# First two k-tiles of the in-projection as plain float32 products, part of the first modulation summed on TensorE, and in-projection passes that run to and fro

## The chip, the cores and the metric

The kernel runs on one core of a Trainium2 chip. The metric is the device time of one execution in microseconds (us). TensorE (PE in the rows) does the matrix products, VectorE (DVE) and ScalarE (ACT) do the elementwise work, GpSimd (POOL) a little of it, and SyncE (SP) issues nearly all DMA transfers. Weights come from HBM; products are summed in the eight banks of PSUM, and everything else lives in SBUF.

## The reference, cut to what matters

One transformer block on 256 tokens of width 2048, all in float32, with modulation vectors computed from a condition vector `c`:

```
mod = silu(c) @ w_ada + b_ada                       # 2048 x 12288
shift_m, scale_m, gate_m, shift_f, scale_f, gate_f = split(mod, 6)
h = rms_norm(x, pre_norm_mix) * (1 + scale_m) + shift_m
q_n, k_c, v_c, k_s, v_s, k_w, v_w, g_n, q_m, k_m, v_m = split(h @ w_in)   # 2048 x 5656
o = concat(nsa_mixer(...), moba_mixer(...)) @ w_o
x = x + gate_m * rms_norm(o, post_norm_mix)
h = rms_norm(x, pre_norm_ffn) * (1 + scale_f) + shift_f
x = x + gate_f * rms_norm(square(relu(h @ w_up)) @ w_down, post_norm_ffn)
```

The change touches the start: `silu(c)`, `shift_m` and `scale_m`, and `h @ w_in`.

## The kernel before

**Products.** A float32 product runs as three products in the faster fp32r format: each operand is split into a high part (`hi`, a cast on ACT) and the rest (`lo`, a subtraction on DVE), and `products` issues hi x hi, hi x lo and lo x hi. K is cut into 16 k-tiles of 128 rows. The 5656 columns of `w_in` form six blocks: `kv`, `qn`, `qm`, `km`, `vm` of 1024 columns and `kw` of 536. For one k-tile and one block of 1024 columns there are two token tiles x two halves of 512 columns x three products = 12 products; the four sums lie in four PSUM banks. Five banks (`mbank`) serve these sums, three (`bank`) the rest.

**Passes.** All k-tiles cannot run at once, since their modulation is not known yet. So the in-projection runs in passes: k-tiles 0 to 3 of all six blocks, 4 to 7 of all six, 8 to 11 of `qm` and `km`, then 8 to 15 of `kv`, `kw`, `qn`, 12 to 15 of `qm` and `km`, and 8 to 15 of `vm`. After each pass of a block its four banks are evacuated: copied out by ACT the first time, added to the earlier sum by DVE (line 573) after that.

**Modulation.** `mod_units` makes shift and scale for a group of k-tiles (`M_MODS`, four groups of four). Their columns of `w_ada` (4 x 128 for shift, 4 x 128 for scale) are loaded for all 16 k-tiles of `c`, and DVE multiplies each of these 16 blocks of 128 x 1024 by a column of `silu(c)` and adds it up (line 310, a SCALAR_TENSOR_TENSOR). Eight transposes on PE and two sums on DVE (line 347) then add over the partitions, POOL adds the bias and multiplies by the gain (lines 351, 353), ACT applies shift and scale to the transposed x (line 372) and casts the high part, and DVE makes the low part. The groups for the next pass are worked out during a pass (`spread`).

**Order.** `Stream` emits units (a load, a preparation, a use) in a fixed order. Loads go through five buffers of 1 MB (`rawtile`); a buffer is free when the preparation has read it, and SP issues the loads in order, so one load that waits for its buffer holds up all later ones. The five split weight tiles (`whi`, `wlo`) form a second limit. Each engine's own queue is written by a scheduler and runs strictly in order.

Of the kernel before, what the change touches and what calls it, by code (L numbers as in the profile page):

```python
# [12 lines left out]
F32 = mybir.dt.float32  # L13
F32R = mybir.dt.float32r
# [61 lines left out]
class Stream:  # L76
    """Emits units in order; loads and preparations run ahead as far as the buffers reach."""
# [56 lines left out]
def spread(base, extra, first, last):  # L134
    """The units of base with the groups in extra placed between positions first and last."""
# [17 lines left out]
def tile_adaln_block(ctx: ExitStack, tc: tile.TileContext, x, c, w_ada, b_ada, g_pm, g_qm, w_in,  # L153
# [28 lines left out]
    # Constants  # L182
    ident = cp.tile([P, P], F32, name="ident")
    make_identity(nc, ident)
    onesr = cp.tile([P, P], F32R, name="onesr")
    nc.scalar.activation(onesr, ident, AF.Identity, bias=1.0, scale=0.0)
    identb = cp.tile([P, P], BF16, name="identb")
    nc.vector.tensor_copy(identb, ident)
    sel4 = cp.tile([P, 32], F32, name="sel4")
    nc.vector.tensor_add(sel4, ident[:, 0:32], ident[:, 32:64])  # L190
    nc.vector.tensor_add(sel4, sel4, ident[:, 64:96])
    nc.vector.tensor_add(sel4, sel4, ident[:, 96:128])
    mhalf = cp.tile([P, 1], F32, name="mhalf")
    nc.gpsimd.memset(mhalf, -0.5)

    maskf = accp.tile([P, NT, NCMP + T], F32, tag="acc", name="maskf")
    nc.gpsimd.memset(maskf, 0.0)
    for t in range(NT):
        nc.gpsimd.affine_select(
            out=maskf[:, t, 0:NCMP], in_=maskf[:, t, 0:NCMP], compare_op=ALU.is_ge, fill=NEG,  # L200
            base=t * P - (CLEN - 1), pattern=[[-CSTR, NCMP]], channel_multiplier=1)
        nc.gpsimd.affine_select(
            out=maskf[:, t, NCMP:], in_=maskf[:, t, NCMP:], compare_op=ALU.is_ge, fill=NEG,
            base=t * P, pattern=[[-1, T]], channel_multiplier=1)
    mask = cp.tile([P, NT, NCMP + T], BF16, name="mask")
    nc.vector.tensor_copy(mask, maskf)

    rp = cp.tile([P, NT, 2, HD], F32, name="rp")

# [7 lines left out]
    nc.scalar.dma_start(stageb[0:32, :], ck_pos[0])  # L217
    nc.scalar.dma_start(stageb[32:64, :], cv_pos[0])
# [7 lines left out]
    cola = cp.tile([P, P], F32, name="cola")  # L226
    colb = cp.tile([P, 80], F32, name="colb")
    pc = bank("pconst0")
    nc.tensor.transpose(pc[:, 0:16], stagec, ident[0:16, 0:16])
    nc.scalar.copy(colb[:, 0:16], pc[:, 0:16])  # L230
    pb = bank("pconst")
    nc.tensor.transpose(pb[:, 0:64], stageb, ident[0:64, 0:64])
    nc.scalar.copy(colb[:, 16:80], pb[:, 0:64])
    pa = bank("pconst2")
    nc.tensor.transpose(pa[:, 0:P], stagea, ident)
    nc.scalar.copy(cola, pa[:, 0:P])
    for i in (1, 4):
        scale = cola[:, i * KD:(i + 1) * KD]
# [1021 lines left out]
```

## Time and profile before

| | us |
|---|---|
| time, three runs | 1200.81, 1201.71, 1202.43 (median 1201.71) |
| span of the profiled execution, first to last instruction | 1199.2 |
| TensorE busy | 1140.5 (95%) |
| VectorE busy | 908.5 (76%) |
| ScalarE busy | 602.2 (50%) |
| DMA | 312 MB, 260 GB/s on average |

The profiled execution is listed by its span alone; the median of the timed runs is 2.5 us above it. Busy shares are averages over stages with different limits. The in-projection fills about the first 280 us; the output projection and the FFN follow, and there TensorE is busy nearly all the time.

### The profile page before, as it was taken

To read this page: it belongs to the slowest core of one execution; us is meant where nothing else is said; L and a number is where in the kernel's file an instruction comes from. 1 tells how busy PE (TensorE), PEld (TensorE's weight loads), DVE (VectorE), ACT (ScalarE), POOL (GpSimd) and SP (SyncE) were. 2 spreads that over 40 slices of the span, in tenths; PEclk is the share of its full clock that TensorE was granted. 3 is DMA by queue.
4 is the path that set the end of the run, shared out by engine and by line. 5 is a ranking of instruction groups with operands and counts; after the bars stand their busy time and mean duration, and the time that the engine had idled before them with its cause. 6 is when DMAs were issued, how large, how long until landed. Compare 5 with 4: busy or idle time off the path is not lost.

```text
span 1199.2 us, 14451 instructions
## 1 busy us (share of the span) xinstructions
PE 1140.5 (95%) x5429; PEld 935.9 (78%) x5429; DVE 908.5 (76%) x1086; ACT 602.2 (50%) x922; POOL 32.7 (3%) x38
## 2 busy tenths in 40 slices
PE   2599998999999999999999999999999999999997
PEld 1477886878778887888888788888888888888885
DVE  6877999879998897876988986757666666665564
ACT  3446343436756666665343344767544444444441
POOL 1000001000000031000000000000000000000000
PEclk9699999999999999999999999999999999999999
DMA  9898989886766695997867875555677767775541
GB/s 334 311 392 277 361 307 336 261 293 246 273 223 233 246 356 178 360 333 276 315 250 279 315 266 193 176 176 187 215 258 268 259 253 274 253 278 178 207 142 70
DMA packets 88249, 312.02 MB, mean 260 GB/s; under 512 B 6051, under 2 KB 6515, under 8 KB 75251
## 3 DMA queue, kind: packets, MB, share of 16 engines
q1 hardware_dynamic: 87876, 311.01, 72.6%
q8 instruction: 42, 0.69, 0.2%
q14 instruction: 27, 0.21, 0.0%
q10 hardware_dynamic: 304, 0.11, 0.0%
HBM read 308.99 MB, written 2.10 MB: 259 GB/s over the span
## 4 chain that ended last, share of the span: by engine, by line
PE 81%; DVE 9%; issue 3%; DMA 3%; ACT 2%; POOL 1%; DVEq 0%; POOLq 0%; ACTq 0%
PE dps L498 9%; PE dps L496 9%; PE dps L497 9%; PE up L496 9%; PE up L498 9%; PE up L497 9%; DVE modm L310 3%; PE wo L496 2%; PE wo L498 2%; PE wo L497 2%; PE ft L1083 1%; PE in_vm L497 1%; PE in_vm L498 1%; PE in_vm L496 1%; PE in_kv L496 1%
## 5 line engine op out<-in xcount | busy, mean ns | idle before, releaser
L310 DVE SCALAR_TENSOR_TENSOR modf<-modf,csil,modf 128x1024 f32<-128x1024 f32 x60 | 76.7, 1278 | 9.2 <-DMA modf<-in_w_ada_dram 9.1
L310 DVE SCALAR_TENSOR_TENSOR modm<-modm,csil,modm 128x1024 f32<-128x1024 f32 x60 | 76.8, 1280 | 0.9
L1099 DVE TENSOR_TENSOR facc<-up,facc 128x512 f32<-128x512 f32 x96 | 61.5, 683 | 18.7 <-PE up L498 18.7
L310 DVE SCALAR_TENSOR_TENSOR gatef<-gatef,csil,gatef 128x1024 f32<-128x1024 f32 x32 | 40.6, 1278 | 1.3 <-DMA gatef<-in_w_ada_dram 1.3
L310 DVE SCALAR_TENSOR_TENSOR gatem<-gatem,csil,gatem 128x1024 f32<-128x1024 f32 x32 | 40.2, 1273 | 0.0
L1139 DVE TENSOR_TENSOR flo<-facc,fhi 128x512 fp32r<-128x512 f32 x32 | 21.7, 684 | 2.0 <-ACT fhi L1138 2.0
L1138 ACT CAST fhi<-facc 128x512 fp32r<-128x512 f32 x32 | 19.7, 624 | 5.3 <-PE up L497 1.9
L1101 ACT ACTIVATE facc<-facc 128x512 f32<-128x512 f32 x32 | 18.4, 624 | 2.8 <-DVE facc L1099 2.8
L1097 ACT COPY facc<-up 128x512 f32<-128x512 f32 x32 | 17.8, 594 | 1.6 <-PE up L498 1.0
L492 DVE TENSOR_TENSOR up_13lo<-up,up_13hi 128x1024 fp32r<-128x1024 f32 x8 | 9.8, 1226 | 11.5 <-ACT up_13hi L491 11.5
L492 DVE TENSOR_TENSOR up_14lo<-up,up_14hi 128x1024 fp32r<-128x1024 f32 x8 | 9.8, 1224 | 11.1 <-ACT up_14hi L491 11.1
L345 PE MATMUL modm0t<-ident,modm 128*128 128x128 f32 x8 | 1.9, 424 | 17.0 <-DVE modm L310 17.0
L1088 ACT ACTIVATE facc<-ft 128x512 f32<-128x512 f32 x32 | 17.2, 588 | 0.4 <-PE ft L1083 0.2
L1083 PE MATMUL ft<-ident,facc 128*128 128x128 f32 x128 | 16.8, 273 | 0.0
L1083 PEld LDWEIGHTS ft<-ident,facc 128*128 128x128 f32 x128 | 14.7, 140 | 2.6 <-ACT facc L1088 0.5
L492 DVE TENSOR_TENSOR up_0lo<-up,up_0hi 128x1024 fp32r<-128x1024 f32 x8 | 9.8, 1223 | 7.7 <-ACT up_0hi L491 7.7
L491 ACT CAST up_7hi<-up 128x1024 fp32r<-128x1024 f32 x8 | 8.4, 1056 | 14.3 <-PE up L498 14.3
L491 ACT CAST up_11hi<-up 128x1024 fp32r<-128x1024 f32 x8 | 8.4, 1055 | 14.2 <-PE up L498 14.2
L351 POOL TENSOR_TENSOR modf0red<-modf0red,cola 128x8 f32<-128x8 f32 x1 | 9.0, 8993 | 227.3 <-ACT wo_15hi L491 227.3
L491 ACT CAST up_10hi<-up 128x1024 fp32r<-128x1024 f32 x8 | 8.4, 1056 | 13.3 <-PE up L498 13.3
L491 ACT CAST up_6hi<-up 128x1024 fp32r<-128x1024 f32 x8 | 8.4, 1055 | 13.3 <-PE up L498 13.3
L345 PEld LDWEIGHTS modm0t<-ident,modm 128*128 128x128 f32 x8 | 1.6, 224 | 17.2 <-ACT in_kv_1hi L491 17.2
(2340 smaller groups left out, 4020.2 us busy)
## 6 DMA issues: line engine op xcount, KB each, us to landing
up<-in_w_up_dram SPq DMA_DIRECT2D x64, 1024.0 KB, 6.6
dn<-in_w_down_dram SPq DMA_DIRECT2D x64, 1024.0 KB, 4.9
modm<-in_w_ada_dram SPq DMA_DIRECT2D x64, 512.0 KB, 6.5
modf<-in_w_ada_dram SPq DMA_DIRECT2D x64, 512.0 KB, 5.9
gatem<-in_w_ada_dram SPq DMA_DIRECT2D x16, 1024.0 KB, 4.9
wo<-in_w_o_dram SPq DMA_DIRECT2D x16, 1024.0 KB, 5.3
gatef<-in_w_ada_dram SPq DMA_DIRECT2D x16, 1024.0 KB, 4.8
in_kv<-in_w_in_dram SPq DMA_DIRECT2D x8, 1024.0 KB, 7.3
```

Source lines behind the costliest of these rows:

```text
L310: nc.vector.scalar_tensor_tensor(part, w[:, j:j + step], csil[:, k:k + 1], part, ALU.mult, ALU.add)
L491: nc.scalar.copy(hi[:, 0:n], src)
L492: nc.vector.tensor_sub(lo[:, 0:n], src, hi[:, 0:n].bitcast(F32))
L496: nc.tensor.matmul(o, shi, whi, start=first, stop=False)
L497: nc.tensor.matmul(o, shi, wlo, start=False, stop=False)
L498: nc.tensor.matmul(o, slo, whi, start=False, stop=last)
L1083: nc.tensor.transpose(b[:, (2 * i + t) * P:(2 * i + t + 1) * P], f[:, t, (2 * j + i) * P:(2 * j + i + 1) * P], ident)
L1097: nc.scalar.copy(dst, b)
L1099: nc.vector.tensor_add(dst, b, dst)
L1101: nc.scalar.activation(dst, dst, AF.Relu)
L1138: nc.scalar.copy(hi, f)
L1139: nc.vector.tensor_sub(lo, f, hi.bitcast(F32))
```

## The change

- `M_MODS` becomes (2, 2, 4, 4, 4). The first two groups are two k-tiles wide, so their blocks are 128 x 512; four k-tiles of `c` share one buffer, loaded by four DMAs of 256 KB in place of two of 512 KB.
- In the first group the blocks of k-tiles 3, 7, 11, 13 and 15 of `c` (`M_DIRECT`) are not added on DVE: TensorE multiplies them by the column of `silu(c)` (`column_sums`), which adds over the partitions at once. All groups of the mixer now end with such products by a column of ones instead of transposes, with the bias added by one more product, and two small DVE operations follow. The later FFN groups keep the transposes, with bias and gain on DVE instead of POOL.
- k-tiles 0 and 1 (`M_PLAIN` = 2) of all blocks are multiplied as plain float32: no cast, no subtraction, one product in place of three. Their loaded buffer is held until TensorE has used it.
- The passes are now: k-tiles 0 and 1 of `kv`, `kw`, `qn`, `vm`, `km`, `qm`; then 2 and 3 in the order `qm` (its banks kept from the pass before), `km`, `vm`, `qn`, `kw`, `kv`; then `kv` on through 4 to 7 in the same banks, `kw`, `qn`, `vm`, `km`, and `qm` 4 to 11 in one go, `km` 8 to 11. From `kv` 8 to 15 on the order is that of before.
- At the start the constants for the mixer (mask, `sel4`, compressed positions) are loaded and made later, and the path from `c` to `silu(c)` is shorter.

```
-M_MODS = (4, 4, 4, 4)
+M_MODS = (2, 2, 4, 4, 4)
+M_PLAIN = 2
+M_DIRECT = (3, 7, 11, 13, 15)
...
                 for kk in range(krows):
                     k = i * krows + kk
                     w = st["raw"][:, kk * n:(kk + 1) * n]
+                    if direct is not None and k in M_DIRECT:
+                        direct(k, w)
+                        continue
...
+        def column_sums(w, v, stop):
+            if "b" not in sums:
+                sums["b"] = bank(f"{name}t")
+                nc.tensor.matmul(sums["b"][:, 0:2 * nk].rearrange("p (s k) -> p s k", s=2), ident,
+                                 bias[:, :, ks], start=True, stop=False, skip_group_check=True)
+            for i in range(2 * nk):
+                nc.tensor.matmul(sums["b"][:, i:i + 1], w[:, i * P:(i + 1) * P], v,
+                                 start=False, stop=stop, skip_group_check=True)
...
+                column_sums(acc.t, one, True)
+                b = sums["b"]
+                nc.vector.tensor_mul(red[:, nk:], b[:, nk:2 * nk], gcol[:, ks])
+                nc.vector.tensor_copy(red[:, 0:nk], b[:, 0:nk])
...
+                        if k < plain:
+                            nc.tensor.matmul(b[:, 0:wd], s32,
+                                             raw[:, kk * ncol + off:kk * ncol + off + wd],
+                                             start=first, stop=last)
+                        else:
+                            products(b[:, 0:wd], shi, slo, whi[:, cs], wlo[:, cs], first, last)
...
+    turn0 = in_units("qm", 0, 4)
+    turn1 = in_units("kv", 2, 8)
+    turn2 = in_units("qm", 4, 12)
+    stream.add(flat(mods[0]))
+    base = flat(in_units(n, 0, 2) for n in ("kv", "kw", "qn", "vm", "km")) + turn0[:2]
+    stream.add(spread(base, mods[1], 3, len(base) - 1))
+    base = turn0[2:] + flat(in_units(n, 2, 4) for n in ("km", "vm", "qn", "kw")) + turn1[:2]
+    base.insert(3, Unit(None, late_constants))
+    stream.add(spread(base, mods[2], 0, len(base) - 2))
+    base = turn1[2:] + flat(in_units(n, 4, 8) for n in ("kw", "qn", "vm", "km")) + turn2[:4]
+    stream.add(spread(base, mods[3], 0, len(base) - 5))
+    base = turn2[4:] + in_units("km", 8, 12)
```

Three places show how the queues move. The first is TensorE's queue from the last transposes of x to the first products of the in-projection (`modm0t` is the bank of the first modulation group, `xnm` the modulated x, `in_kv_0_0` the bank of the first half of `kv` for the first token tile). Before:

```order
L274 MATMUL xt_3_269<-ident,x_150 128x128 x4
L345 MATMUL modm0t_316<-ident,modm_192 128x128 x4
L345 MATMUL modm0t_322<-ident,modm_192 128x128 x4
L496 MATMUL in_kv_0_0_346<-in_kv_0hi,modm0hi_332 128x512
L497 MATMUL in_kv_0_0_346<-in_kv_0lo,modm0hi_332 128x512
L498 MATMUL in_kv_0_0_346<-in_kv_0hi,modm0lo_333 128x512
```

After the change the same place reads:

```order
L283 MATMUL xt_3_280<-ident,x_121 128x128 x4
L359 MATMUL modm0t<-csil,modm_138 128x1 x4
L356 MATMUL modm2t<-cola,ident 128x4
L359 MATMUL modm0t<-csil,modm_143 128x1 x4
L359 MATMUL modm0t<-csil,modm_148 128x1 x8
L359 MATMUL modm0t<-one,modm_175 128x1 x4
L497 MATMUL in_kv_0_0_306<-in_kv_0_153,xnm_211 128x512
L497 MATMUL in_kv_1_0_308<-in_kv_0_153,xnm_211 128x512
```

The eight transposes have become products with one column, and the first product of the in-projection reads the loaded weight and x directly.

The second place is SP's queue, from the loads of the first modulation group to the sixth load of weights or modulation behind it (`modm` is modulation, `in_kv`, `in_kw` and so on are weights of the in-projection). Before:

```order
L295 DMA modm_205<-in_w_ada_dram 128x2x512 x2
L433 DMA in_kv_0_246<-in_w_in_dram 128x2x1024
L433 DMA in_kv_2_278<-in_w_in_dram 128x2x1024
L433 DMA in_kw_0_282<-in_w_in_dram 128x2x536
L295 DMA modm_286<-in_w_ada_dram 128x2x512 x2
L433 DMA in_kw_2_291<-in_w_in_dram 128x2x536
L295 DMA modm_301<-in_w_ada_dram 128x2x512 x2
```

After:

```order
L305 DMA modm_148<-in_w_ada_dram 128x2x256 x4
L476 DMA in_kv_0_153<-in_w_in_dram 128x2x1024
L476 DMA in_kw_0_185<-in_w_in_dram 128x2x536
L305 DMA modm_194<-in_w_ada_dram 128x2x256 x4
L305 DMA modm_206<-in_w_ada_dram 128x2x256 x4
L476 DMA in_qn_0_257<-in_w_in_dram 128x2x1024
L305 DMA modm_292<-in_w_ada_dram 128x2x256 x4
L476 DMA in_vm_0_318<-in_w_in_dram 128x2x1024
```

The group ahead of the first product is four buffers of 1 MB instead of eight (before, `modm_157` to `modm_205`), and weights of one pair of k-tiles alternate with the next group.

The third place is where the plain pass ends: `km` 0 and 1 is the pass's fifth block, `qm` 2 the first weights that are split. ACT's queue there, after the change:

```order
L629 COPY km_441<-in_km_0_1_411 128x512
L629 COPY km_444<-in_km_1_1_413 128x512
L544 CAST in_qm_2hi<-in_qm_2_384 128x1024
L544 CAST in_qm_3hi<-in_qm_2_384 128x1024
L544 CAST in_km_2hi<-in_km_2_450 128x1024
```

And DVE's queue at the same place, after the change (`modm_415` is the sum of the third group):

```order
L323 SCALAR_TENSOR_TENSOR modm_415<-modm_363,csil,modm_415 128x1024
L545 TENSOR_TENSOR in_qm_2lo<-in_qm_2_384,in_qm_2hi 128x1024
L323 SCALAR_TENSOR_TENSOR modm_415<-modm_404,csil,modm_415 128x1024
L545 TENSOR_TENSOR in_qm_3lo<-in_qm_2_384,in_qm_3hi 128x1024
L323 SCALAR_TENSOR_TENSOR modm_415<-modm_404,csil,modm_415 128x1024
L323 SCALAR_TENSOR_TENSOR modm_415<-modm_418,csil,modm_415 128x1024 x2
L545 TENSOR_TENSOR in_km_2lo<-in_km_2_450,in_km_2hi 128x1024
L323 SCALAR_TENSOR_TENSOR modm_415<-modm_454,csil,modm_415 128x1024
L545 TENSOR_TENSOR in_km_3lo<-in_km_2_450,in_km_3hi 128x1024
L323 SCALAR_TENSOR_TENSOR modm_415<-modm_454,csil,modm_415 128x1024
L631 TENSOR_TENSOR km_441<-in_km_0_0_561,km_441 128x512
L323 SCALAR_TENSOR_TENSOR modm_415<-modm_469,csil,modm_415 128x1024 x2
```

The casts stand behind the copies that evacuate `km`, so DVE's second row there waits for TensorE to finish that block; and the first addition of a bank (line 631) now stands between two steps of the third group's sum.

## Rows read from the trace of the kernel before

**Rows 1.** The page: busy time by engine; TensorE's granted clock by slice.

```profile
PE 1140.5 (95%) x5429; PEld 935.9 (78%) x5429; DVE 908.5 (76%) x1086; ACT 602.2 (50%) x922; POOL 32.7 (3%) x38
PEclk9699999999999999999999999999999999999999
```

**Rows 2.** Windows: stretch, length, busy time by engine, granted clock, DMA share, GB/s.

```profile
15.00:38.00 23.00, 5.66 (x34) 4.97 (x33) 21.36 (x20) 6.88 (x18) 1.59 (x1) 0.72 1.04 392
50.00:123.00 73.00, 69.53 (x329) 57.01 (x328) 57.89 (x55) 38.79 (x57) 2.17 (x2) 1.00 0.93 337
123.00:200.00 77.00, 72.90 (x341) 59.38 (x340) 75.07 (x81) 29.58 (x32) 2.18 (x2) 1.00 0.92 337
200.00:250.00 50.00, 47.33 (x271) 39.83 (x273) 45.01 (x77) 21.67 (x30) 4.01 (x3) 1.00 0.77 255
250.00:1100.00 850.00, 846.28 (x4042) 693.82 (x4041) 643.60 (x770) 454.81 (x712) 16.71 (x13) 1.00 0.72 257
```

**Rows 3.** Timeline from the start to the first products: start, duration, instruction.

```profile
4.98 2.13 SPq L519 DMA_DIRECT2D x<-in_x_dram  x4
9.72 1.06 ACT L525 ACTIVATE xj<-x 128x1024 f32<-128x1024 f32 x1 [4.78 <-DMA x<-in_x_dram]
14.98 0.74 DVE L305 TENSOR_SCALAR modm<-modm,csil 128x1024 f32<-128x1024 f32 x1
...
37.42 1.94 PE L345 MATMUL modm0t<-ident,modm 128*128 128x128 f32 x8 [17.00 <-DVE modm L310]
44.59 0.79 PE L496 MATMUL in_kv<-in_kv_0hi,modm0hi 128*128 128x512 f32 x1 [5.24 <-ACT modm0hi L375]
48.94 0.39 PE L497 MATMUL in_kv<-in_kv_0lo,modm0hi 128*128 128x512 f32 x1
```

**Rows 4.** TensorE's timeline at two places: plain float32 products, then fp32r products.

```profile
316.95 0.59 PE L743 MATMUL on<-pt,ksv 128*128 128x256 f32 x2
317.38 0.38 PE L744 MATMUL on<-pt,ksv 128*128 128x128 f32 x2
...
274.78 0.39 PE L496 MATMUL in_qm<-in_qm_13hi,modm12hi 128*128 128x512 f32 x1
275.01 0.39 PE L497 MATMUL in_qm<-in_qm_13lo,modm12hi 128*128 128x512 f32 x1
```

**Rows 5.** DVE's timeline between 121 and 201 us, cut to one row of each kind.

```profile
121.81 0.69 DVE L573 TENSOR_TENSOR kcv<-in_kv,kcv 128x512 f32<-128x512 f32 x1 [0.39 <-PE in_kv L498]
130.94 1.46 DVE L573 TENSOR_TENSOR wide<-in_kw,wide 128x268 f32<-128x268 f32 x4
132.32 1.21 DVE L492 TENSOR_TENSOR in_qn_6lo<-in_qn,in_qn_6hi 128x1024 fp32r<-128x1024 f32 x1
133.45 1.27 DVE L310 SCALAR_TENSOR_TENSOR modm<-modm,csil,modm 128x1024 f32<-128x1024 f32 x1
134.64 1.22 DVE L492 TENSOR_TENSOR in_qn_7lo<-in_qn,in_qn_7hi 128x1024 fp32r<-128x1024 f32 x1
155.72 0.69 DVE L376 TENSOR_TENSOR modm8lo<-xnm,modm8hi 128x512 fp32r<-128x512 f32 x1 [1.62 <-ACT modm8hi L375]
166.96 0.74 DVE L305 TENSOR_SCALAR modm<-modm,csil 128x1024 f32<-128x1024 f32 x1
198.00 1.22 DVE L492 TENSOR_TENSOR in_km_11lo<-in_km,in_km_11hi 128x1024 fp32r<-128x1024 f32 x1
```

**Rows 6.** TensorE's timeline where `kv` 8 begins.

```profile
199.57 0.39 PE L497 MATMUL in_km<-in_km_11lo,modm8hi 128*128 128x512 f32 x1
202.50 0.39 PE L496 MATMUL in_kv<-in_kv_8hi,modm8hi 128*128 128x512 f32 x1
```

**Rows 7.** ScalarE's timeline: one cast of a weight, one copy of a bank.

```profile
44.95 1.03 ACT L491 CAST in_kv_2hi<-in_kv 128x1024 fp32r<-128x1024 f32 x1
...
55.75 0.59 ACT L571 COPY kcv<-in_kv 128x512 f32<-128x512 f32 x1
```

**Rows 8.** Window of 2 us in which loads with runs of 512 B (`w1k`) land.

```profile
238.00:240.00 2.00, 2.00 (x15) 1.80 (x14) 2.00 (x6) 1.08 (x2) 0.00 (x0) 1.00 1.06 292
```

More of the change, by code (lines that the diff above doesn't have):

```diff
@@ L180, in rawtile, with sigmoid_parts @@
         return wp.tile([P, 2048], F32, tag="raw", bufs=RAWBUFS, name=name)
+    def sigmoid_parts(dst, src):
+        nc.vector.tensor_scalar(dst, src, -87.0, None, ALU.max)
+        nc.scalar.activation(dst, dst, AF.Exp, scale=-1.0)
+        nc.vector.tensor_scalar(dst, dst, 1.0, None, ALU.add)
     ident = cp.tile([P, P], F32, name="ident")
     make_identity(nc, ident)
[L185 to L192, printed above, removed]
     mhalf = cp.tile([P, 1], F32, name="mhalf")
     nc.gpsimd.memset(mhalf, -0.5)
[L196 to L208, printed above, removed]
+    one = cp.tile([P, 1], F32, name="one")
+    nc.gpsimd.memset(one, 1.0)
+    cola = cp.tile([P, P], F32, name="cola")
+    colb = cp.tile([P, 64], F32, name="colb")
+    csil = cp.tile([P, KD], F32, name="csil")
     stagea = accp.tile([P, P], F32, tag="acc", name="stagea")
@@ L277, in transposed, with gemv_units @@
                                b[:, j * 256:(j + 1) * 256].rearrange("p (k q) -> p k q", k=2))
-    def gemv_units(name, c0, width, both, krows, acc, first):
+    def gemv_units(name, c0, width, both, krows, acc, first, direct=None):
         units = []
@@ L334, in first @@
                 acc.t = gp.tile([P, 2 * W], F32, tag="ga", name=name)
-        units = gemv_units(name, base + k0 * P, W, True, 2 if W <= 512 else 1, acc, first)
+        ks = slice(k0, k0 + nk)
+        sums = {}
+        def column_sums(w, v, stop):
[6 more added lines that the diff above has]
+                                 start=False, stop=stop, skip_group_check=True)
@@ new lines, in reduce @@
+            if tag == "f" and k0:
+                with tc.high_priority():
+                    for i0 in range(0, 2 * nk, 4):
+                        n = min(4, 2 * nk - i0)
+                        b = bank(f"{name}t{i0}")
+                        for i in range(n):
+                            nc.tensor.transpose(b[:, i * P:(i + 1) * P],
+                                                acc.t[:, (i0 + i) * P:(i0 + i + 1) * P], ident)
+                        nc.vector.tensor_reduce(red[:, i0:i0 + n],
+                                                b[:, 0:n * P].rearrange("p (k q) -> p k q", k=n),
+                                                axis=AX.X, op=ALU.add)
+                    nc.vector.tensor_add(red.rearrange("p (s k) -> p s k", s=2),
+                                         red.rearrange("p (s k) -> p s k", s=2), bias[:, :, ks])
+                    nc.vector.tensor_mul(red[:, nk:], red[:, nk:], gcol[:, ks])
+                return lambda k: (red[:, k - k0:k - k0 + 1], red[:, nk + k - k0:nk + k - k0 + 1])
@@ L569, in done @@
                 dst = acc[n][:, t, :]
-            if g == 0:
+            if (name, ci, t) not in begun:
+                begun.add((name, ci, t))
                 nc.scalar.copy(dst, b[:, 0:wd])
@@ L908, in tile_adaln_block @@
     mods = [mod_units("m", k0, n, xnm, hstat) for k0, n in zip(k0s, M_MODS)]
-    stream.add([x_units(0), x_units(1)])
+    xu = [x_units(0), x_units(1)]
+    columns()
+    stream.add(xu)
     gm = gate_units("m", g_qm, gate_m)
```

170 lines of the change are left out of this document (86 added, 84 removed).

## The prediction

> **What bounds the kernel now.** I read the page first: TensorE is busy for 95% of the span and at its full clock in every slice of 30 us but the second [rows 1]. So there is little to win except where TensorE stands still, and the windows say where that is. From 250 to 1100 us it is busy for 846 of 850 us; up to 38 us it has hardly begun; from 50 to 250 it loses 3.5, 4.1 and 2.7 us in the three stretches [rows 2]. The change touches nothing after the in-projection that TensorE waits for, so I ask one question: how much earlier does TensorE reach a place behind which both programs are alike? That place is the first product of `kv` 8, at 202.50 us [rows 6].
>
> Next I looked for what sets the pace up to there. The timeline of the start shows the sum of the first modulation group: DVE begins it at 14.98, TensorE waits for it 17 us, sums at 37.42 and has its first product at 44.59 [rows 3]. In that stretch DVE is busy for 21.4 of 23 us while DMA moves 392 GB/s [rows 2]. So the first sum is paced by DVE, with DMA close behind.
>
> From 50 to 123 us all three are fairly full, none quite: DVE 57.9 of 73, TensorE 69.5 [rows 2]. From 123 to 200 DVE is busy for 75.1 of 77 us [rows 2]. There each of its instructions starts about 0.08 us before its predecessor ends (132.32 + 1.21 against 133.45, 133.45 + 1.27 against 134.64) [rows 5]: this queue has no room. The split of `km` 11 ends at 199.22 [rows 5] and TensorE uses it at 199.57 [rows 6]. **DVE, not TensorE, sets when `kv` 8 begins**, though over the whole kernel it is busy for only 76% [rows 1]. That decides the estimate: an earlier start of TensorE is worth only what DVE can follow.
>
> **The start.** The first group now needs half the bytes: 4.2 MB of `w_ada` and 2.1 MB of x. At 392 GB/s [rows 2] that is 16.1 us; with some 2.5 us until the stream runs (an estimate: the first x took 4.7 us from issue at 4.98 to use at 9.72 [rows 3], and fewer constants stand ahead of it now) the last block lands near 18.5. DVE has 11 of the 16 blocks, half as wide, so about 0.65 us each in place of 1.27 [rows 5]: 7 us, which now hides behind the loads. Behind the last block come one DVE step (0.7), four column products (I take 1 us: eight transposes took 1.94 [rows 3]; between 0.3 and 2), two small DVE operations (0.3), one ACT or DVE step for the modulation (0.6, as for k-tile 0 alone), and a margin of 1.4 for late DVE work on x. First product at about 22.5 instead of 44.59; bounds 20.5 and 26.
>
> The loads are the open term. Their runs are 1 KB instead of 2 KB, and each transfer is 256 KB. The nearest row is the load with runs of 512 B, which moved 292 GB/s [rows 8], against 392. At that rate 4.2 MB take 3.7 us longer, so the start lies between 22.5 and 26. I take 22.5, since 1 KB is nearer in kind to the 2 KB loads, of which many were in flight. Beside this, the Trainium skill ("DMA: Bandwidth & Descriptors", section Bandwidth, Measured) advises transfers of at least 1 MiB and gives 341 GB/s for 1 MB and 138 for 64 KB. By it these loads would be well below 341: at 250 GB/s, my estimate between its two figures, 6.3 MB would take 9 us longer than at 392. The 512 KB loads of this trace, at 392 GB/s [rows 2], already beat its figure for 1 MB.
>
> **The plain pass.** A plain float32 product appears as two instructions. For 256 columns they take 0.43 us (316.95 to 317.38) [rows 4], so 512 columns cost 0.86 and 268 cost 0.45. An fp32r product of 512 columns takes 0.23 (274.78 to 275.01) [rows 4], three of them 0.68. Pass one has 40 sums of 512 and 8 of 268: 40 x 0.86 + 8 x 0.45 = 38.0 us, against some 30 before. So TensorE pays 8 us more; at the end of the chain this costs nothing as long as DVE is the later one. The clock starts at the lower level: before, products were slow from 44.59 and reached 0.39 us at 48.94 [rows 3], 4 us at half speed. That adds 2 us. The pass ends at 22.5 + 38 + 2 = 62.5.
>
> In this pass DVE loses time. The loaded buffers now wait for TensorE (6.9 us for each MB of weights), no weights are split, and DVE's queue holds only the second group (16 half-wide steps, some 10 us) and the beginning of the third. Then it stands at the split of `qm` 2, whose cast waits on ACT's queue behind the copies of `km` (third place of the order). `km` ends 6.9 us before the pass, at 55.6; a copy is 0.6 and a cast 1.0 [rows 7], so DVE goes on at 57.2. Up to the first addition (line 631) it has four splits and six steps: 4 x 1.13 + 6 x 1.19 [rows 5] = 11.7 and a little for steps on the same tile, 69.1. TensorE finishes that bank after `qm` 2 and 3 and a quarter of `km` (5.4 + 1.4), at 69.3. So DVE passes this point at 69.3.
>
> **From there to `kv` 8.** Counted in DVE's queue, from that addition up to the split of `km` 11: 37 steps of the modulation x 1.19 = 44.0; two first steps x 0.66 = 1.3; 34 splits x 1.13 = 38.4; six of 536 columns x 0.63 = 3.8 (by width); 32 additions x 0.64 = 20.5; eight of 268 columns x 0.36 = 2.9; four low parts of x, 2.4; four small ones, 0.6; steps on the same tile, 0.8. Durations are those of [rows 5], less the 0.08 of overlap. The sum is 114.7. The same sum made for the kernel before between 132.32 and 198.00 [rows 5] (21 splits, 20 steps, one first step, 20 additions, two low parts, two reductions) gives 63.7 and, with the wait of 1.62 [rows 5], 65.3 against 65.68 measured. So the method holds.
>
> For waits I take those of before: 0.39 + 1.62 [rows 5] in 77 us [rows 2], so 3.0 in 114.7. The split of `km` 11 then ends at 69.3 + 114.7 + 3.0 = 187.0 and `kv` 8 begins 3.3 us later, as it did (199.22 to 202.50), at 190.3. **That is 12.2 us earlier than 202.50.**
>
> TensorE does not forbid it: from 62.5 it has 38 k-tiles of 1024 columns x 2.72 (12 x 0.227) and six of `kw` x 1.45, 112 us, and would be there at 175 if nothing held it. DMA does not either: 43 MB remain at 62 us, 110 us at 392 GB/s. So some 15 us of TensorE's earlier start turn into waits for DVE, spread over 62 to 190.
>
> **What costs nothing.** The 12 casts saved on ACT: ACT is 50% busy [rows 1] and is not waited for. The cheaper last step of each group (two small DVE operations for two reductions and two POOL operations): some 1 us of DVE each, contained in the count above. The FFN's groups with bias and gain on DVE: under 1 us in all, in a stretch where TensorE is at 846 of 850 [rows 2]. Behind `kv` 8 both programs have the same work, so the 12.2 us pass to the end: the span becomes 1199.2 - 12.2 = 1187.0, and with the 2.5 us by which the median lies above the span, **1189.5**.
>
> **Rivals.** (a) *TensorE and DVE hold each other up.* Blocks are now two k-tiles long in the second pass (5.4 us of products), and four banks must be evacuated in each, by a DVE whose additions stand between modulation steps; with five banks TensorE waits for DVE's addition and DVE for TensorE's last product in turn. Between 69 and 187 us eleven blocks are evacuated on DVE. At 0.4 us of DVE wait each, the only such wait seen [rows 5], the cost is 4.4, about my allowance of 3. At 1.4 us each it is 15.4, allowance and gain are gone (1201.9), and beyond that the change loses: at 2.2 us each the time would be 1189.5 + 24.2 - 3.0 = 1210.7. Against it: DVE lost only 2 us of 77 before with the same five banks.
> (b) *Slow small loads.* The start is at 26 and, as all later terms hang on it, the time is 1193; with 9 us, 1198.5.
> (c) *DVE runs ahead better.* Between 24 and 69 us I give DVE some 23 us of work (second group, three steps of two of the third, four splits), so it idles for 22. If the buffers let it do 5 to 7 us more of the third group there, the time is 1182 to 1185; TensorE's own floor at 175 gives 1174.
> (d) *It does nothing.* The 22 us of idle in the plain pass are what the change pays for starting early; before, DVE idled some 15 us in the whole stretch from 50 to 123 [rows 2]. If that idle time is 12 us larger, because a load waits for a buffer that TensorE still reads and all loads behind it wait too, `kv` 8 stays at 202 and the time at 1201.7.
>
> **Chances and range.** The forecast (gain 8 to 16 us) 0.50; (c) 0.15; (b) and mild cases of (a) and (d), with gains of 2.4 to 8, 0.16; (a) and (d) with no measurable change 0.10; slower 0.09. A measurement here can tell about 0.2%, 2.4 us, from no change. So faster 0.81, same 0.10, slower 0.09. The range leaves out the far end of (c) and most of the cases without a gain: 1182 to 1200.
>
> **What would show it.** Right: first product near 22.5; plain sums 0.86 apart; a DVE that idles from 25 to 57 and is full from 70; `kv` 8 near 190; TensorE with some 15 us of new waits for DVE between 62 and 190. Wrong: a first product after 26; waits of DVE for `in_*` banks above 10 us in sum; DVE already full during the plain pass; a granted clock that stays at the lower level in it; or an end that moves by less than `kv` 8 does.

## The result, and the profile after

The changed kernel takes 1213.6 us (median of 4 runs, 1212.98 to 1218.75) against 1201.3 before: the ratio is 1.0115, with a 95% interval of 1.0094 to 1.0135. A gain of 12 us was forecast; it lost 12. The profiled execution of the changed kernel is the longest of its four (1218.75, span 1217.0; the spans of the others are 1211.2 to 1211.8).

The page, lines that answer to [rows 1]:

```profile
PE 1175.2 (97%) x5473; PEld 952.3 (78%) x5473; DVE 895.5 (74%) x1104; ACT 591.5 (49%) x908; POOL 13.3 (1%) x23
PEclk9998999999999999999899999999999999999999
```

TensorE is busier than before and the kernel is slower. 8 us more of TensorE time were meant (the plain products); some of the rest is the lower clock, in the fourth slice and in the twentieth.

Windows, with the columns of [rows 2]; the last row runs to the first product of `kv` 8:

```profile
15.00:38.00 23.00, 21.99 (x80) 16.96 (x81) 15.43 (x24) 4.99 (x14) 2.02 (x4) 1.00 1.01 343
50.00:123.00 73.00, 64.26 (x233) 42.91 (x232) 50.19 (x58) 27.85 (x42) 0.00 (x0) 0.91 0.85 299
123.00:200.00 77.00, 75.30 (x357) 61.90 (x355) 71.52 (x78) 28.98 (x34) 0.00 (x0) 1.00 0.96 344
200.00:250.00 50.00, 48.13 (x264) 41.58 (x265) 43.15 (x59) 20.86 (x28) 1.81 (x1) 1.00 0.81 276
250.00:1100.00 850.00, 840.74 (x4013) 689.26 (x4012) 644.17 (x795) 451.53 (x710) 5.16 (x5) 0.99 0.73 255
0.00:211.60 211.60, 188.43 (x773) 140.88 (x774) 156.71 (x196) 76.40 (x117) 5.95 (x16) 0.97 0.91 320
```

From 50 to 123 us TensorE now stands still for 9 us (3.5 before), and 250 to 1100, which was to stay as it was, loses 9.3 in place of 3.7.

TensorE's timeline at the places of [rows 3] and [rows 6]: the end of the first modulation group, the first product, the end of the plain pass, `kv` 8.

```profile
22.68 5.26 PE L359 MATMUL modm0t<-csil,modm 128*128 128x1 f32 x24
27.80 1.84 PE L359 MATMUL modm0t<-one,modm 128*128 128x1 f32 x8
...
30.66 9.37 PE L497 MATMUL in_kv<-in_kv,xnm 128*128 128x512 f32 x16 [1.01 <-ACT xnm L414]
...
43.48 7.03 PE L497 MATMUL in_qn<-in_qn,xnm 128*128 128x512 f32 x16
...
71.44 0.79 PE L549 MATMUL in_qm<-in_qm_2hi,modm2hi 128*128 128x512 f32 x1
...
211.63 1.12 PE L549 MATMUL in_kv<-in_kv_8hi,modm8hi 128*128 128x512 f32 x4
```

So the first product came at 30.66 in place of 44.59: 14 us earlier, if not the 22 that were forecast. The plain pass took 40.8 us, and a block of eight plain products 6.87 (43.48 to 50.35; the first such block took 9.2), 0.86 each, as forecast. And yet `kv` 8 begins at 211.63, 9.1 us later than before. TensorE took 181.0 us from its first product to there, where the kernel before took 157.9. The other part of the loss lies behind `kv` 8: 1005.4 us to the end against 996.7. As this execution is the longest by 5 us, the first part is probably overstated: in two runs below that are edited behind `kv` 8 alone, `kv` 8 begins at 206.84 and 207.90, 4.3 and 5.4 us later than before.

The second pass (k-tiles 2 and 3) is where the start is given back. SyncE's, ScalarE's, DVE's and TensorE's timelines there:

```profile
73.02 0.41 SPq L476 DMA_DIRECT2D in_vm<-in_w_in_dram  x1
...
82.29 1.05 ACT L544 CAST in_vm_2hi<-in_vm 128x1024 fp32r<-128x1024 f32 x1 [10.15 <-DMA in_vm<-in_w_in_dram]
84.20 1.54 ACT L629 COPY qm<-in_qm 128x512 f32<-128x512 f32 x3
...
85.71 1.22 DVE L545 TENSOR_TENSOR in_vm_3lo<-in_vm,in_vm_3hi 128x1024 fp32r<-128x1024 f32 x1
88.04 0.69 DVE L631 TENSOR_TENSOR km<-in_km,km 128x512 f32<-128x512 f32 x1
...
88.78 0.80 PE L549 MATMUL in_km<-in_km_2hi,modm2hi 128*128 128x512 f32 x1 [4.38 <-DVE km L631]
89.80 0.63 PE L551 MATMUL in_km<-in_km_2hi,modm2lo 128*128 128x512 f32 x1
```

Read from the bottom: TensorE waits 4.4 us for a bank, which DVE's addition frees; that addition stands behind the splits of `vm` 2 and 3; those wait for ScalarE's casts; and these wait 10 us for a load that was issued at 73.02 and landed at 82.3. ScalarE's copies of the `qm` banks stand behind the same cast. After the wait the products start 0.43 us apart in place of 0.23: they do so up to 96.4 us, and the granted clock is 0.70 from 80 to 97 us.

### The profile page after: what moved, and what is told of

It reads as the page before. It is cut to its first block, busy times and chain, and to the rows that moved or that the text cites. A ratio compares the mean times of both kernels' runs of the same rounds, so it can differ in the third digit from the quotient of the medians.

```text
span 1217.0 us, 14522 instructions
## 1 busy us (share of the span) xinstructions
PE 1175.2 (97%) x5473; PEld 952.3 (78%) x5473; DVE 895.5 (74%) x1104; ACT 591.5 (49%) x908; POOL 13.3 (1%) x23
## 4 chain that ended last, share of the span: by engine, by line
PE 87%; DVE 6%; DMA 4%; issue 2%; ACT 1%; SPq 0%; POOL 0%; DVEq 0%; POOLq 0%; ACTq 0%
PE dps L551 10%; PE dps L549 10%; PE dps L550 10%; PE up L550 9%; PE up L551 9%; PE up L549 9%; PE wo L550 2%; PE wo L549 2%; PE wo L551 2%; DMA modf<-in_w_ada_dram 2%; DVE modm L323 1%; PE ft L1137 1%; PE in_vm L549 1%; PE in_vm L550 1%; PE in_vm L551 1%
## 5 line engine op out<-in xcount | busy, mean ns | idle before, releaser
L323 DVE SCALAR_TENSOR_TENSOR modm<-modm,csil,modm 128x1024 f32<-128x1024 f32 (+1 forms) x70 | 76.6, 1094 | 7.8 <-DMA modm<-in_w_ada_dram 6.6
L545 DVE TENSOR_TENSOR up_13lo<-up,up_13hi 128x1024 fp32r<-128x1024 f32 x8 | 9.8, 1224 | 11.6 <-ACT up_13hi L544 11.6
L1142 ACT ACTIVATE facc<-ft 128x512 f32<-128x512 f32 x32 | 17.1, 587 | 0.4 <-PE ft L1137 0.2
L544 ACT CAST up_5hi<-up 128x1024 fp32r<-128x1024 f32 x8 | 8.4, 1054 | 16.3 <-PE up L551 13.0
L549 PE MATMUL up<-up_4hi,modf4hi 128*128 128x512 f32 x32 | 13.3, 417 | 3.0 <-DVE facc L1153 3.0
L550 PE MATMUL up<-up_1lo,xmhi 128*128 128x512 f32 x32 | 13.2, 412 | 2.6 <-DVE up_1lo L545 2.6
L544 ACT CAST up_14hi<-up 128x1024 fp32r<-128x1024 f32 x8 | 8.4, 1049 | 12.6 <-PE up L551 12.6
```

The lines of the kernel that those rows point to most:

```text
L323: nc.vector.scalar_tensor_tensor(part, w[:, j:j + step], csil[:, k:k + 1], part, ALU.mult, ALU.add)
L544: nc.scalar.copy(hi[:, 0:n], src)
L545: nc.vector.tensor_sub(lo[:, 0:n], src, hi[:, 0:n].bitcast(F32))
L549: nc.tensor.matmul(o, shi, whi, start=first, stop=False)
L550: nc.tensor.matmul(o, shi, wlo, start=False, stop=False)
```

## The experiments

Each line is one profiled execution (first product of the in-projection, first of `kv` 8, span) and the timed runs; the ratio is to the kernel before, run on the same chip. "kv 8 to end" is the span less the start of `kv` 8.

"Column blocks" are the blocks of the first modulation group that TensorE multiplies by the column of `silu(c)`, five in the changed kernel.

| kernel | first | kv 8 | kv 8 to end | median | ratio, 95% |
|---|---|---|---|---|---|
| before | 44.59 | 202.50 | 996.7 | 1201.3 | 1 |
| changed | 30.66 | 211.63 | 1005.4 | 1213.6 | 1.0094 to 1.0135 |
| two column blocks | 27.74 | 208.83 | 1001.8 | 1213.5 | 1.0072 to 1.0113 |
| split 0, 1 | 28.05 | 206.53 | 1002.5 | 1211.2 | 1.0067 to 1.0097 |
| additions first | 27.84 | 206.48 | 1008.1 | 1218.7 | 1.0115 to 1.0171 |
| `vm` casts on GpSimd | 29.95 | 210.32 | 1004.6 | 1213.4 | 1.0065 to 1.0123 |
| `qm` casts on DVE | 27.32 | 203.84 | 1003.8 | 1215.7 | 1.0086 to 1.0144 |
| FFN ends as before | 26.75 | 207.90 | 996.4 | 1208.4 | 1.0046 to 1.0076 |
| first FFN end only | 28.02 | 206.84 | 995.8 | 1205.7 | 1.0027 to 1.0055 |
| half the steps | 28.63 | 210.14 | 1004.0 | 1214.6 | 1.0091 to 1.0125 |
| half the loads | 26.88 | 192.57 | 1004.1 | 1199.4 | 0.9978 to 1.0003 |
| combination 1 | 29.64 | 208.32 | 996.4 | 1206.7 | 1.0029 to 1.0059 |
| combination 2 | 28.12 | 210.19 | 996.2 | 1209.4 | 1.0061 to 1.0086 |
| warm start | 33.12 | 212.70 | 1000.3 | 1216.0 | 1.0117 to 1.0147 |
| passes of before | 29.54 | 208.83 | 996.0 | 1206.6 | 1.0038 to 1.0063 |
| the same, plain | 28.24 | 203.11 | 996.4 | 1200.8 | 0.9993 to 1.0012 |
| before, half the steps | 44.02 | 205.26 | 997.2 | 1202.2 | 0.9997 to 1.0018 |
| before, half the loads | 44.02 | 195.77 | 997.2 | 1194.3 | 0.9930 to 0.9960 |

Eight of these leave the start as the change has it; their first product lies between 26.75 and 30.66, so differences of 4 us in "first" and "kv 8" between two single executions say little.

**Single edits of the in-projection.** The first moves column products back to DVE:

```
-M_DIRECT = (3, 7, 11, 13, 15)
+M_DIRECT = (3, 7)
```

> Only k-tiles 3 and 7 of the first group go to TensorE; 11, 13 and 15 are summed on DVE. In the changed kernel DVE ends its share of that sum at 23.1 us, while TensorE, with 32 transposes of x and 40 column products at 0.21 us each, is ready at 29.6 and makes its first in-projection product at 30.66. Theory A (the start is late because TensorE has more to do there than DVE): DVE ends near 25.3, the column by ones follows, first product near 28.2, and the end moves by about the same 2.5 us: 1211 us. Rival (the loads, not TensorE, set the start): first product stays within 0.7 us of 30.66 or comes later, time 1213 to 1215.

First product at 27.74: DVE ended at 24.8, the columns by ones followed, as Theory A has it, but this lies within the spread of the unedited start, and the time is unchanged. The second splits k-tiles 0 and 1 again:

```
-M_PLAIN = 2
+M_PLAIN = 0
```

> k-tiles 0 and 1 are split again as hi and lo (three fp32r products), all else as changed. Theory A (the plain pass costs by holding loaded buffers until TensorE is through with them, 21 us of SyncE's waits before 70 us, so that later loads come late; and by 8 us more of TensorE): the pass ends near 62 in place of 71.4, the load of vm 2 lands before 78 in place of 82.3, kv 8 begins 4 to 8 us before 211.6, time 1206 to 1210. Rival B (DVE is the bound and the plain pass spares it 12 splits, 13.6 us): kv 8 begins at 212 or later, time 1213 to 1222.

`vm` 2 landed at 76.6 and `kv` 8 came at 206.53, both as Theory A expected, though 206.53 is within the spread of the unedited start; TensorE's waits for `km` stayed at 6.1 us and the time fell by only 2.4, to 1211.2, above the range of Theory A. The next two change who stands behind whom, in the evacuation of banks and in `split`:

```
-                nc.vector.tensor_add(dst, b[:, 0:wd], dst)
+                with tc.high_priority():
+                    nc.vector.tensor_add(dst, b[:, 0:wd], dst)
```

> The additions that evacuate banks on DVE get priority, so that a block's four additions stand together and ahead of steps of the modulation in DVE's queue; work unchanged. Theory A (TensorE's 6.6 us of waits for km banks between 78 and 89 us come from ScalarE, whose copies of the qm banks stand behind a cast that waits for the late load of vm 2): no gain, the same waits, time 1211 to 1216. Rival B (the additions come too late in DVE's own queue): waits of TensorE for additions shrink below 2 us, time 1205 to 1209.

```
-        nc.scalar.copy(hi[:, 0:n], src)
+        if name in ("in_vm2_2", "in_vm2_3"):
+            nc.gpsimd.tensor_copy(hi[:, 0:n], src)
+        else:
+            nc.scalar.copy(hi[:, 0:n], src)
...
-        nc.scalar.copy(mask, maskf)
+        nc.gpsimd.tensor_copy(mask, maskf)
```

> The casts of vm 2 and vm 3 and the one of the mask go from ScalarE to GpSimd, which is idle there, so ScalarE's queue no longer holds the copies of the qm banks behind a cast that waits for a load. Theory A: the qm copies run at 75 to 79 in place of 84.2 to 86.8, TensorE's waits for km fall from 6.6 to under 2 us, the granted clock stays at its upper level through 80 to 110, and kv 8 begins 4 to 7 us before 211.6: 1207 to 1210 us. Rival B (DVE's queue is what holds the km banks): waits and time as before this edit, 1212 to 1215.

With the additions first, waits for `km` fell to 3.7 us (5.1 with the next one, of `vm` for the last `km` addition), and the time rose by 5, to 1218.7. `kv` 8 came at 206.48, no later than in other runs; what the profile shows of the rise lies behind it (1008.1 us to the end, with 5.2 us of waits for casts of `up` 1). Neither range was met. With the casts on GpSimd the copies of `qm` ran at 74.8 to 77.4, as Theory A wanted, and TensorE's waits for `km` were 7.7 us all the same: Theory A fell, and Rival B of that run was met in waits and time (1213.4). What held the banks there was DVE's queue, whose splits of `vm` stood behind the load, which landed at 81.7.

**Is it the load, or DVE's work?** Three edits. The first takes a wait of DVE away (6.9 us for casts of `qm` 2 and 3, which stood behind copies on ScalarE):

```
+        if name in ("in_qm0_2", "in_qm0_3"):
+            nc.vector.tensor_copy(hi[:, 0:n], src)
```

> The casts of qm 2 and qm 3 go from ScalarE to DVE, which otherwise waits 6.9 us for them, since they stand behind copies of km banks in ScalarE's queue. Theory S (supply: buffers come free late in the plain pass, so the load of vm 2 lands at 82.3 us and what stands behind it holds TensorE up): the load of vm 2 lands before 78, TensorE's waits for km fall from 6.6 to under 3 us, kv 8 begins at 203 to 208, time 1206 to 1210. Rival L (load on DVE: between 67 and 92 us its queue has more to do than TensorE's products give time for, whatever lands when): waits of 5 us or more, kv 8 at 209 to 213, time 1211 to 1215.

This one settles nothing: `kv` 8 at 203.84 and the load at 77.7 as Theory S has it, waits of 5.8 us as Rival L has it, and a median no better than the changed kernel's. The other two leave out half of the third group's sum, first the steps alone, then their loads too:

```
+                    if name == "modm4" and k % 2:
+                        continue
```

> Leaves out every second step of the third modulation group's sum (8 of 16 steps of 1.19 us, so shift and scale of k-tiles 4 to 7 are of half the sum); the loads stay. Rival L (DVE has too much to do in the second pass): TensorE's waits for km fall from 6.6 to under 2 us, kv 8 begins 6 to 10 us earlier, at 201 to 206, time 1204 to 1208. Theory S (supply): vm 2 still lands at 79 or later, waits of 4 us or more stay, kv 8 at 207 to 211, time 1209 to 1214.

```
                 for kk in range(krows):
+                    if name == "modm4" and kk % 2:
+                        continue
                     nc.sync.dma_start(v[:, kk], src[:, kk])
```

> As the run with half the steps of the third modulation group's sum left out, but their loads are left out too (4 MB of 8; shift and scale of k-tiles 4 to 7 are of half the sum). From the first in-projection product to the first of kv 8 the changed kernel takes 181.0 us; half the steps alone changed that by +0.5. Theory S (loads come too late in the second pass): vm 2 lands 44 us or less behind the first product in place of 51.6, TensorE's waits for km fall under 3 us, and the 181.0 become 171 to 176. Rival O (the order of the queues, ScalarE's copies behind casts and DVE's additions behind splits, whatever lands when): 178 us or more.

TensorE's waits from 60 to 130 us, half the steps:

```profile
PE in_vm L551 <- DVE km L633: 3.7, 1, 3.7
PE in_km L551 <- DVE km L633: 2.4, 3, 0.8
PE in_kw L551 <- DVE qn L633: 1.1, 1, 1.1
```

The same, half the loads, and ScalarE's row there:

```profile
PE in_km L553 <- ACT qm L633: 1.3, 1, 1.3
...
73.48 1.05 ACT L548 CAST in_vm_2hi<-in_vm 128x1024 fp32r<-128x1024 f32 x1 [5.59 <-DMA in_vm<-in_w_in_dram]
```

9.5 us of DVE's work less: nothing gained, and the wait moved from `km` to `vm`. 4.2 MB of loads less on top of that: the load of `vm` 2 lands 46.6 us behind the first product in place of 51.6 (not the 44 expected), the waits for DVE's additions of `km` are gone, 165.7 us from the first product to `kv` 8 in place of 181.0 (less than the 171 expected at best), and 15 us off the time. The number of buffers is the same in both runs: a buffer of 1 MB holds two of the group's k-tiles, and one of the two stays out. Rival L is out; the loads set the pace of the second pass.

**Was that so before the change too?** The prediction read DVE as the pace-setter up to `kv` 8. The same two cuts in the kernel before, in the group that is summed from 113 to 155 us (`modm8` in place of `modm4`):

> The kernel before, with every second step of its third modulation group's sum left out (k-tiles 8 to 11; 8 of 16 steps of 1.19 us on DVE, within the stretch from 113 to 155 us), so that shift and scale there are of half the sum; all loads stay. The prediction held that DVE sets when kv 8 begins (202.5): then 8 x 1.19 = 9.5 us of DVE's work less brings kv 8 to 193 to 196 and the time to 1191 to 1195. If the loads set it (67.2 MB go through DMA before kv 8, at 332 GB/s and 91% of its engines' time): kv 8 at 200 to 203, time 1198 to 1202.

> As the run before it, but the loads of those 8 blocks are left out too (4.2 MB of 67.2). If the loads set when kv 8 begins: 4.2 MB at 293 to 332 GB/s, 12.6 to 14.3 us, kv 8 at 188 to 191, time 1186 to 1190. If DVE does: no more than the steps alone gave, 193 to 196. If neither does and TensorE is close behind: kv 8 at 196 to 202 in both.

Windows of the two runs, steps alone above and loads too below:

```profile
123.00:200.00 77.00, 72.68 (x334) 59.45 (x333) 68.42 (x74) 29.42 (x32) 0.40 (x2) 0.97 0.91 326
...
123.00:200.00 77.00, 76.89 (x368) 64.21 (x367) 73.60 (x81) 34.05 (x39) 2.63 (x5) 1.00 0.91 324
```

Without the steps DVE is no longer full (68.4 of 77) and nothing is gained, which refutes the prediction's reading: `kv` 8 at 205.26, later than either range, and the time 0.9 us above the kernel before. Without the loads `kv` 8 comes at 195.77 and the time falls by 6.9 us: less than the 12 to 14 expected, because TensorE, at 76.9 of 77 us, is then the bound itself. It had stood still for no more than 7.6 us from 50 to 200 in the kernel before [rows 2].

TensorE is as close behind in the changed kernel. Windows from the first product to `kv` 8 with half the loads, in the changed kernel and in the kernel before:

```profile
26.88:192.57 165.69, 161.40 (x687) 120.00 (x688) 133.38 (x156) 64.67 (x88) 0.77 (x1) 0.99 0.92 331
...
44.02:195.77 151.75, 148.27 (x696) 122.97 (x697) 131.18 (x136) 75.02 (x96) 2.76 (x5) 0.99 0.89 318
```

With the loads eased in both, TensorE starts 17.1 us earlier, has 13.1 us more to do up to `kv` 8, and reaches it 3.2 us earlier, in two single executions. That speaks against the 12 us even with faster loads.

**What makes the loads late?** The bytes before `kv` 8, by windows from 0 to its start, in the kernel before, the changed one with its first FFN end undone (below), the short start with the passes of before (below), and the one with half the loads:

```profile
0.00:202.50 202.50, 158.94 (x739) 129.90 (x740) 168.90 (x182) 88.60 (x131) 11.50 (x21) 0.94 0.91 332
...
0.00:206.80 206.80, 181.30 (x773) 134.68 (x774) 156.76 (x196) 76.19 (x117) 5.94 (x16) 0.98 0.93 328
...
0.00:203.10 203.10, 177.69 (x749) 132.30 (x750) 153.71 (x187) 76.26 (x117) 5.97 (x16) 0.96 0.94 331
...
0.00:192.60 192.60, 177.50 (x774) 134.45 (x775) 147.04 (x188) 76.84 (x117) 6.02 (x16) 0.98 0.93 330
```

Length times rate: 67.2, 67.8, 67.2 and 63.6 MB. The same product for all sixteen kernels with whole loads gives 67.2 to 68.3 MB at 318 to 333 GB/s, with DMA busy for 90 to 94% of the time, whenever TensorE starts. The last experiments keep the short start and go back to the passes of before, first with all weights split, then with k-tiles 0 and 1 plain:

```
-    turn0 = in_units("qm", 0, 4)
-    turn1 = in_units("kv", 2, 8)
...
+    head = in_units("kv", 0, 4)
+    stream.add(flat(mods[0]) + head[:2])
+    stream.add(flat(mods[1]))
+    base = head[2:] + flat(in_units(n, 0, 4) for n in ("kw", "qn", "qm", "km", "vm"))
...
+    base = flat(in_units(n, 4, 8) for n in ("kv", "kw", "qn", "qm", "km", "vm"))
```

> Keeps the short start of the change (first group two k-tiles wide, k-tiles 3 and 7 as column products, late constants), but goes back to the passes of the kernel before (k-tiles 0 to 3 of all blocks, then 4 to 7, and so on), splits all weights, and ends the first FFN group with transposes. Theory S (the passes of two k-tiles ask for more bytes in their time than DMA brings: 8 MB of modulation beside 5.7 MB of weights in the second one, while the first leaves DMA idle): with 8 MB beside 11.4 MB as before the loads keep up; first product near 28, k-tile 2 of kv at 42 to 45, kv 8 at 196 to 200, 996 us from there to the end: 1194 to 1199 us, faster than both kernels. Rival (whatever TensorE starts earlier is lost to DVE, which is full from 113 to 200 us already before): kv 8 at 201 to 204, 1199 to 1203.

> As the run with the short start and the passes of before, but k-tiles 0 and 1 as plain float32 products: TensorE has 8 us more to do in the first pass, DVE 12 splits (13.6 us) less, and buffers are held until TensorE is through. If DVE sets the pace up to kv 8: kv 8 up to 6 us earlier than without, 1190 to 1196. If TensorE and the held buffers do: kv 8 4 to 8 us later than without, 1199 to 1206.

The short start alone takes 1206.6 us, with `kv` 8 at 208.83: slower than the kernel before and slower than either expectation, so Theory S fell as well. With plain products it is as fast as the kernel before, no faster (0.9993 to 1.0012), though TensorE begins 16 us earlier; `kv` 8 came 5.7 us earlier than without, as the case for DVE has it, and the time lies in the range of the other case. Here the plain products gain 5.8 us, where in the change taking them away gained 2.4; why they help here was not isolated.

**The loss behind `kv` 8.** It begins at the seam from the output projection to the FFN. All FFN groups ended as before (transposes, bias and gain on GpSimd), then only the first group's column products undone (`tag == "f" and k0` becomes `tag == "f"`, DVE keeps bias and gain):

> Only the ends of the FFN's modulation groups go back to what they were: eight transposes, sums on DVE, bias and gain on GpSimd. In the changed kernel and the four runs made of it the time from the first product of kv 8 to the end is 1002 to 1008 us, against 996.7 before, and it is lost at the seam from the output projection to the FFN. Theory C (these ends, small as they are, cause it): back to 996 to 999 us from kv 8 to the end, time 1205 to 1209. Rival D (the seam is only ordered otherwise by the scheduler, since everything ahead of it has moved): still 1001 to 1008, time 1211 to 1216.

> As the run with the FFN groups ended as before, but bias and gain stay on DVE: only the first FFN group's column products go back to transposes. If the column products of the first FFN group bring the loss at the seam: 996 to 999 us from kv 8 to the end. If the two operations on DVE in place of GpSimd do, through the order of the queues that the scheduler makes of them: 1001 to 1008.

Both give 996 us from `kv` 8 on, as before the change. TensorE in the changed kernel, at the seam and, in the last row, 100 us behind it:

```profile
476.52 1.50 PE L1099 MATMUL x2t<-ident,xa 128*128 128x128 f32 x12 [1.18 <-issue]
479.26 0.50 PE L549 MATMUL up<-up_0hi,xmhi 128*128 128x512 f32 x1 [1.24 <-ACT xmhi L417]
485.74 0.79 PE L550 MATMUL up<-up_1lo,xmhi 128*128 128x512 f32 x1 [2.55 <-DVE up_1lo L545]
486.33 0.63 PE L551 MATMUL up<-up_1hi,xmlo 128*128 128x512 f32 x1
...
588.78 0.80 PE L549 MATMUL up<-up_4hi,modf4hi 128*128 128x512 f32 x1 [2.97 <-DVE facc L1153]
```

And with the first FFN end undone:

```profile
469.63 1.50 PE L1099 MATMUL x2t<-ident,xa 128*128 128x128 f32 x12 [1.14 <-issue]
470.89 0.48 PE L550 MATMUL wo<-wo_15lo,othi 128*128 128x512 f32 x1
472.71 0.50 PE L549 MATMUL up<-up_0hi,xmhi 128*128 128x512 f32 x1 [0.42 <-ACT xmhi L417]
...
481.32 0.50 PE L550 MATMUL up<-up_1lo,xmhi 128*128 128x512 f32 x1 [0.51 <-DVE up_1lo L545]
```

In the second, products of `wo` 15 are kept back behind the transposes and cover ScalarE's work on `xmhi`; in the first they have all been run before, TensorE waits 1.24 and 2.55 us, and then its products start 0.43 us apart up to 489 us. The seam is the smaller part: at 588.78 TensorE waits 2.97 us for an addition on DVE, which had itself stood 3.80 us for a load of the second FFN group, and its products start 0.43 us apart up to 595. This wait lasts 0 to 3.2 us in the nine kernels with these column products, which take 1000.3 to 1008.1 us behind `kv` 8, and at most 0.6 in the nine without, which take 995.8 to 997.2. The edit shows that the first group's column products bring the loss; why the order of the queues turns on them, and why that load comes later, was not isolated.

**Combinations, and a try at the clock.** Combination 1: all weights split, two column blocks, FFN ends as before.

> k-tiles 0 and 1 split again, two column products blocks instead of five, FFN groups ended as before. If what the single edits showed adds up: kv 8 at 203 to 206.5 (206.53 with the split alone), and with Theory C 997 to 999 us from there to the end, time 1202 to 1207. With Rival D 1001 or more from there, time 1207 to 1212. Either way not clearly faster than the kernel before.

Combination 2: FFN ends as before, two column blocks, `qm` casts on DVE, and the third group's loads begin behind those of `qm` 2 and `km` 2:

```
-    stream.add(spread(base, mods[2], 0, len(base) - 2))
+    stream.add(spread(base, mods[2], 4, len(base) - 2))
```

> What helped or was meant to, together: FFN groups ended as before, two column product blocks in place of five, casts of qm 2 and 3 on DVE, and the loads of the third group begin behind those of qm 2 and km 2, so that vm 2 has three of them ahead in place of five. From the single edits: first product at 27 to 28.5, 174 to 177.5 us from there to kv 8 (176.5 with the casts alone), 996.5 to the end: span 1198 to 1202, time 1200 to 1204. If the casts on DVE gave nothing by themselves, as the median of their timed runs says (1215.7): 181 us, time 1206 to 1209.

The first met the range of time for a cured seam (1206.7), though `kv` 8 came at 208.32; the second took 182 us from the first product to `kv` 8, the 181 of no effect at all. TensorE's waits for `km` were gone there and 5.4 us of waits for `qn` had come; that a load moved ahead makes others late is the likely reason, and was not shown. The try at the clock put 20 transposes of the identity ahead of `columns()`:

> Twenty more transposes of the identity (results unused) run on TensorE between 3.5 and 8.5 us, where it waits for DMA, so that it has worked before its first real products. In the changed kernel column products take 0.21 us an instruction at 21 to 28 us and 0.12 later on. If the lower clock is what makes the start late: column products at 0.12 us from the first, first in-projection product at 24.5 to 26.5 in place of 26.8 to 30.7, and 2 to 5 us off the time: 1208 to 1211. If the clock does not follow from this: first product at 27 or later, 1213.

Inconclusive: `cola` came late (TensorE waited 6.2 us for it), the first product at 33.12, and the column products still began at 0.21 us.

## Why the prediction was wrong

The steps in their order, by the name each has in the text.

- **"DVE, not TensorE, sets when `kv` 8 begins": wrong, and the step that failed.** A queue whose instructions follow without a gap [rows 5] was taken for the bound. It is full because its work arrives at that pace: with 8 steps less, `kv` 8 comes no earlier (205.26 against 202.50). The loads set the pace: with half of that group's loads less as well it came at 195.77, where TensorE itself became the bound.
- **"DMA does not either: 43 MB remain at 62 us, 110 us at 392 GB/s": wrong in both numbers, and it hid the bound.** 392 GB/s is the rate of one stretch of 23 us [rows 2]. The changed kernel moved 311 GB/s up to 62 us, so that 48.5 MB remained, and 324 GB/s from there to `kv` 8, with DMA busy for 91%. The rate of 337 GB/s and the shares of 0.93 and 0.92 for the long stretches stood in [rows 2]: at 337, the prediction's own 43 MB take 128 us, to 190 us, which is its forecast with nothing to spare, and 48.5 MB take 144, to 206. The Trainium skill ("DMA: Bandwidth & Descriptors", section Bandwidth, Measured) gives 341 GB/s for a transfer of 1 MB issued from GpSimd; the prediction set this aside for the 392 of the start, and the 318 to 333 of these runs over 200 us, issued from SyncE, lie nearer to that figure than 392 does.
- **Start at 22.5, bounds 20.5 to 26: a term mis-sized.** "Four column products" at 1 us were the last of twenty-four. DVE had ended its blocks at 23.1 (19.2 in the forecast); TensorE, without a gap from 11.8 us on, needed 5.26 us for the last twelve columns of `silu(c)`, at 0.22 us an instruction, and 1.84 for the four by ones. First product at 26.8 to 30.7 in eight executions. The loads moved 343 GB/s in place of 392 (15 to 38 us), but no engine waited for one in these sums, so rival (b) fell. The time shows no cost of the late start: two column blocks began 2.9 us earlier and took as long (1213.5).
- **Plain pass, 0.86 us a product, 38 us, and a DVE that idles in it: right.** 6.87 us for eight, 40.8 in all.
- **"TensorE does not forbid it", there at 175: mis-sized.** The 112 us from the end of the plain pass to `kv` 8 count weight products alone. With half the loads TensorE was busy there for 120.8 us (67.5 to 192.6), with three sums of columns at 1.8 us each and their bias among it. By this the floor is near 183, not 175; the forecast does not rest on it, but rival (c) does.
- **114.7 us of DVE work from the first addition to `km` 11: right; waits of 3.0: wrong.** It took 128.5 us (78.88 to 207.4), and the waits in it sum to 13.9 (the longest 6.1, for a bank of `vm`), so the work was 114.6. This is the shape of rival (a). That late loads and not five banks alone are behind it is shown for the `km` banks, whose waits went with half the loads, and argued for the rest. Along the forecast's chain `kv` 8 is 21.3 us late in this execution: 8.2 from the start, 1.4 more up to the first addition, 10.8 from there to `km` 11, and 0.9 up to `kv` 8.
- **"Behind `kv` 8 both programs are alike", FFN ends "under 1 us": wrong.** 4 to 11 us in the runs that keep the first FFN group's column products, less than 1 without them.

The loss of 12.3 us divides, by medians and to within half a microsecond, into two terms. 7.9 go to the first FFN group's column products (1213.6 to 1205.7), which a single edit shows. 4.9 go when the passes of before come back beside the plain products (1205.7 to 1200.8, in which the number of column blocks changed too).

Bytes per pass would explain the second term: the first pass moves 5.8 MB of weights and 4.2 MB of modulation while TensorE is busy for 41 us, and its loaded buffers are held, so DMA falls behind (286 GB/s from 30 to 72 us); the second asks for 5.8 and 8.4 MB in some 30 us of products (40 x 0.68 + 8 x 0.36), 470 GB/s. The kernel before asked for 11.6 and 8.4 MB in one pass of 60. But this is argued and not shown, and one pair of runs speaks against it as the whole cause: with all weights split and two column blocks, passes of two k-tiles (combination 1, 1206.7) and the passes of before (1206.6) take the same time; beside the passes, the two differ in where the FFN's bias and gain are made and where the late constants stand. So what the passes cost hangs on the plain products, and the cause of the second term stays open. So does whether a sixth load buffer would help: it was not tried.

## What to carry to other kernels

Before costing an earlier start, multiply out the bytes that must land up to the place it is to move, and divide by the rate of the long stretch, not of the best one; a DMA share of 0.9 is a bound until shown otherwise. A full queue shows who is busy, not who sets the pace: leave out some of its work and, apart from that, some of its loads, and see which one moves the end. And take a change apart at places that it "does not touch" as well: the larger half of this loss was a small edit that acts some 440 us into the kernel.

## What the hardware showed that was not expected

- DMA moved 392 GB/s for 23 us, but 318 to 333 over the 200 us or so up to `kv` 8, at a busy share of 0.90 to 0.94.
- A float32 product with one column appears as two instructions of 0.21 to 0.22 us each at the start and 0.12 later (1.95 us for 16 at 104 us); a 128-column transpose, one instruction, took 0.25 at the start. By the instruction, one column cost nearly as much as 128.
- In the profiled execution of the changed kernel the clock column reads 1.00 from 15 to 38 us, while the first eight plain products took 9.2 us in place of 6.87.
